# Last stage of a two-layer encoder: outputs in other PSUM banks, two scatters in one sum, both halves scaled together

## Chip, cores and metric

The kernel runs on one core of one Trainium2 chip. The metric is the device time of one execution in microseconds (us); lower is better. In one core five engines run side by side, each through its own list of instructions: TensorE (PE in the rows, its weight loads PEld), VectorE (DVE), ScalarE (ACT), GpSimd (POOL) and SyncE (SP), which issues the DMA transfers. They wait for each other through semaphores.

## The reference

The program is a trunk of two layers on 256 tokens of width 1024, in float32. The change concerns the very last part of the second layer, the mixture of experts: each token goes to 2 of 8 experts, and the weighted outputs are added to the residual `x`.

```python
def moe_swiglu(h, router, w1, w3, w2):
    logits = (t @ router)
    top_v, top_i = lax.top_k(logits, TOP_K)            # TOP_K = 2 of 8
    gates = jax.nn.softmax(top_v, axis=-1)
    combine = jnp.sum(jax.nn.one_hot(top_i, N_EXPERTS) * gates[..., None], axis=1)
    for e in range(N_EXPERTS):                         # w1, w3: 1024 x 3584, w2: 3584 x 1024
        out = out + combine[:, e:e + 1] * swiglu(t, w1[e], w3[e], w2[e])
...
x = x + moe_swiglu(h, router[f], moe_w1[f], moe_w3[f], moe_w2[f])
```

## The kernel before, in words

**Weights.** All weights are read from memory once, as a stream of units of 1 MB (`Stream`, L103): 128 partitions x 2048 numbers. SyncE issues the transfer into a `raw` buffer (7 of them). ScalarE rounds the unit into a high part `whi` (L135, 5 buffers), VectorE subtracts it from the unit and gets the low part `wlo` (L153, 4 buffers), and TensorE multiplies with both, so that the sum keeps float32 accuracy. `pieces` (L139) says whether the two do a unit in one instruction of 2048 numbers or in two of 1024; in the expert part (from unit `whole` on) it is one. The transfer of the stream's very last unit is already cut in two (L121). When TensorE has finished a unit, `release` (L162) asks for the subtraction 4 units ahead and the rounding 5 units ahead.

**Experts.** The tokens of an expert are gathered into up to 128 rows. A stage (L1076) computes the up projections (`h1`, `h3`) of one expert, chunk by chunk, and between them the down projection of the expert before (`down`, L1086), whose two output banks `y0` and `y1` hold 128 x 512 each. Two units are used for each of the 7 chunks of a down projection, so 14 units. For an expert with few tokens ("narrow", at most 64; the last one is) a unit takes 8 matmuls of 512 columns: 2 rows of blocks x (high, low) x (y0, y1). The last stage, `e == NE`, has no up projection: it is only the down projection of the last expert.

**Scatter.** `Back` (L1132) brings an expert's output back to its tokens. `scale` (L1140) multiplies a bank with the gate, on ScalarE into the high part `yh` (L1142) and on VectorE into the low part `yl` (L1143). `scatter` (L1146), for each half `i` of the 1024 columns and each block `b` of 128 tokens, makes two matmuls with the transposed one-hot matrix `pT` (yh at L1149, yl at L1150) and adds the bank to `x` on VectorE (L1151). In the last stage (L1197 to L1208) the scatters of the expert before are put behind the 4th and the 6th unit, and the last unit is done half by half: four matmuls into y0, then `final(0)`: scale, two scatters, two stores (L1153, 256 KB each) on SyncE; then the same for y1.

**PSUM.** The 8 banks are in three rings: four "mm" (`mm_bank`, for h1, h3), two "yd" (`yd_bank`, for y0, y1 and the scatters) and two "tp" (`tp_bank`, for transposes). A ring gives out its oldest bank, and who takes it waits until its last reader is done.

**Order.** In the expert part each engine works through its instructions in the order in which the code is written (`manual_schedule`, L1174); functions given to `in_units(n, fn)` run when n more units are done.

Of the kernel before, what the change touches and what calls it, by code (L numbers as in the profile page):

```python
# [11 lines left out]
F32 = mybir.dt.float32  # L12
F32R = mybir.dt.float32r
I32 = mybir.dt.int32
BF16 = mybir.dt.bfloat16
AF = mybir.ActivationFunctionType
OP = mybir.AluOpType
# [4 lines left out]
P = 128  # L22
D = 1024
KD = D // P
NT = 256
NB = NT // P
DFF = 2816
KF = DFF // P
NE = 8
# [13 lines left out]
GT = 15  # L43
# [26 lines left out]
def kernel(ctx: ExitStack, tc: tile.TileContext, x_in, positions, norm_mix, norm_ffn, conv_in,  # L70
                       conv_w, conv_out, attn_in, q_norm, k_norm, lam_q1, lam_k1, lam_q2, lam_k2, subln,
                       attn_out, ffn_w1, ffn_w3, ffn_w2, router, moe_w1, moe_w3, moe_w2, out):
    nc = tc.nc
    V, S, T = nc.vector, nc.scalar, nc.tensor
# [5 lines left out]
    work = ctx.enter_context(tc.tile_pool(name="work", bufs=2))  # L80
    psum = ctx.enter_context(tc.tile_pool(name="psum", bufs=4, space=PSUM))

    def mm_bank(name="mm"):
        return psum.tile([P, 512], F32, name=name, tag="mm", bufs=4)

    def yd_bank(name="yd"):
        return psum.tile([P, 512], F32, name=name, tag="yd", bufs=2)
# [4 lines left out]
    def tok(b):  # L92
        return slice(b * P, (b + 1) * P)
# [9 lines left out]
    class Stream:  # L103
        def __init__(self, units, whole=0):
            self.units = units
            self.whole = whole
            self.raw = {}
            self.high = {}
            self.spl = {}
            self.nd = 0  # L110
            self.nh = 0
            self.ns = 0
            self.done = 0
# [25 lines left out]
        def pieces(self, i):  # L139
            _, nk, nf = self.units[i]  # L140
            n = nk * nf
            step = n if i >= self.whole else n // 2
            return [slice(c, c + step) for c in range(0, n, step)]

        def split_to(self, j):
# [54 lines left out]
    ECH = DFE // 512  # L200
# [39 lines left out]
    x = const.tile([P, NB, D], F32)  # L240
    xf = x_in.rearrange("o (b p) d -> (o b) p d", p=P)
    outf = out.rearrange("o (b p) d -> (o b) p d", p=P)
# [124 lines left out]
    def proj(outs, xt, w, tsl, first, last, c0=0, cw=None):  # L367

        hi, lo = w
        cw = cw or hi.shape[2] // len(outs)  # L370
        nk = hi.shape[1]
        for kk in range(nk):
            *xs, c = xt(kk)
            a = xs[0][:, c, tsl]
            passes = [(a, hi), (a, lo)] + [(x[:, c, tsl], hi) for x in xs[1:]]
            for j, (l, m) in enumerate(passes):
                for i, o in enumerate(outs):
                    T.matmul(o, lhsT=l, rhs=m[:, kk, c0 + i * cw:c0 + (i + 1) * cw], start=first and kk + j == 0,  # L378
                             stop=last and kk == nk - 1 and j == len(passes) - 1)
# [4 lines left out]
    def chunked(tiles, k0):  # L384
        return lambda k: (*tiles[(k0 + k) // 4], (k0 + k) % 4)
# [59 lines left out]
    with ph1:  # L445
        hh, hl = hpair()
# [31 lines left out]
        for j in range(4):  # L478
# [5 lines left out]
            u = work.tile([P, 2, NT], F32, name="u", tag="w1")  # L484
# [13 lines left out]
            c = slice(2 * (j % 2), 2 * (j % 2) + 2)  # L498
            split(zt[j // 2][0][:, c, :], zt[j // 2][1][:, c, :], z)
            spare(2)  # L500
        u0 = 12
# [16 lines left out]
        hh, hl = hpair()  # L518
# [4 lines left out]
        for part, (n0, n1) in enumerate(FPARTS):  # L523
# [4 lines left out]
            hb, s1b, gt = {}, {}, {}  # L528
# [319 lines left out]
    def in_units(n, fn):  # L848

        pending.append([n, fn])  # L850
# [222 lines left out]
        in_units(2, turn)  # L1073
        return (gp,)

    def stage(s, u0, xs, gt, hooks=(), then=None):  # L1076


        narrow = xs is not None and len(xs) == 1
        hooks = dict(hooks)  # L1080
        full = slice(0, P)
        made = {}
        u = u0
        yb = []

        def down(n):  # L1086
            nonlocal u
            if gt is None:
                return
            if n == 0:  # L1090
                yb.extend([yd_bank("y0"), yd_bank("y1")])
            for i in range(2):
                end = (n, i) == (ECH - 1, 1)
                if end and then:
                    for half in range(2):
                        proj([yb[half]], chunked(gt, 4 * n + 2 * i), s.get(u), full, False, True, half * 512, 512)
                        then(half, yb[half])
                else:
                    proj(yb, chunked(gt, 4 * n + 2 * i), s.get(u), full, n + i == 0, end)
                u += 1  # L1100
                s.release()
                unit_done()

        for n in range(ECH):
            if xs is not None:
                h1, h3 = mm_bank("h1"), mm_bank("h3")
                for which, bank in ((1, h1), (3, h3)):
                    for half in range(2):
                        proj([bank], whole(xs, 4 * half), s.get(u), full, half == 0, half == 1)
                        u += 1  # L1110
                        if which == 1 and half == 1:
                            s1 = work.tile([P, 512], F32, name="s1", tag="w0")
                            S.activation(s1, h1, AF.Copy if narrow else AF.Silu)  # L1113
                        if which == 3 and half == 1:
                            if narrow:
                                s3 = work.tile([P, 512], F32, name="s3", tag="w0")
                                S.activation(s3, h3, AF.Copy)
                                made[n] = activate_narrow(s1, s3)
                            else:
                                made[n] = activate(s1, h3)  # L1120
                        s.release()
                        unit_done()
                        at = (n, 2 * (which // 3) + half)
                        if at in hooks:
                            hooks[at]()
            if n >= LAG:
                down(n - LAG)
        for n in range(ECH - LAG, ECH):
            down(n)
        return u, made, yb  # L1130

    class Back:  # L1132


        def __init__(self, pT, gate):
            self.pT, self.gate = pT, gate
            self.yh = work.tile([P, D], F32R, name="yh", tag="gain", bufs=1)
            self.yl = p3.tile([P, D], F32R, name="yl", tag="yl")

        def scale(self, i, bank):  # L1140
            c = slice(i * 512, (i + 1) * 512)
            S.activation(self.yh[:, c], bank, AF.Copy, scale=self.gate)  # L1142
            V.scalar_tensor_tensor(self.yl[:, c], bank, self.gate, self.yh[:, c].bitcast(F32), op0=OP.mult,  # L1143
                                   op1=OP.subtract)

        def scatter(self, b, i, bank_of=yd_bank, store=False):  # L1146
            c = slice(i * 512, (i + 1) * 512)
            bank = bank_of("sct")
            T.matmul(bank, lhsT=self.pT[:, tok(b)], rhs=self.yh[:, c], start=True, stop=False)  # L1149
            T.matmul(bank, lhsT=self.pT[:, tok(b)], rhs=self.yl[:, c], start=False, stop=True)  # L1150
            V.tensor_tensor(x[:, b, c], bank, x[:, b, c], op=OP.add)  # L1151
            if store:
                nc.sync.dma_start(outf[b][:, c], x[:, b, c])  # L1153

    pe = one_hot(0, slot1, rstds)
    with tc.issue_after(late["S"].ins), tc.issue_after(late["V"].ins):
# [1 line left out]
    xs = gather(pe)  # L1158
# [15 lines left out]
    with tc.manual_schedule(engines={ET.PE, ET.Activation, ET.DVE}):  # L1174
        for e in range(NE + 1):
            box = {}

            def back(b, last=last, bank_of=yd_bank):
                if last is not None:
                    for i in range(2):  # L1180
                        last.scatter(b, i, bank_of)

            def early(e=e):
                if e == 0:
                    some(gates())
                    some(rank_experts())

            def hot(e=e, pe=pe):
                backs[e] = route_back(pe, e, combr, in_units)
                if e + 1 < NE:  # L1190
                    box["pe"] = one_hot(e + 1, slot1 if is_wide(e + 1) else slotn, table=posr)

            def ahead(e=e):
                if e + 1 < NE:
                    box["x"] = gather(box["pe"], in_units) if is_wide(e + 1) else gather_narrow(box["pe"])

            def final(half, bank, box=box):  # L1197
                if half == 0:
                    box["y"] = Back(*backs.pop(NE - 1))
                box["y"].scale(half, bank)  # L1200
                for b in range(NB):
                    box["y"].scatter(b, half, mm_bank, store=True)

            if e == NE:
                in_units(4, lambda: back(0, bank_of=mm_bank))
                in_units(6, lambda: back(1, bank_of=mm_bank))
            u0, gt, yb = stage(st, u0, xs, gt, {(0, 0): early, (0, 3): lambda: back(0), (1, 3): lambda: back(1),
                                                (4, 0): hot, (5, 1): ahead}, final if e == NE else None)  # L1208
            if 0 < e < NE:
                last = Back(*backs.pop(e - 1))  # L1210
                for i in range(2):
                    last.scale(i, yb[i])
            pe, xs = box.get("pe"), box.get("x")
# [182 lines left out]
```

## Time and profile before

| | us |
|---|---|
| median of 3 runs (all: 1341.34, 1343.12, 1349.6) | 1343.12 |
| the profiled execution | 1343.34 |
| its span, first to last instruction | 1341.6 |
| mean granted TensorE clock, share of full speed | 0.993 |

The profile is of one execution. Rows give the start from the beginning of the span and the duration, both in us; x4 at the end of a row means four instructions in a row merged into one. An instruction's row tells the engine, the line of the kernel, the operation, and what is written from what is read, by the names in the program. In brackets stands the idle time of the engine just before, and whose result ended it. Matmul durations run from the start to the result; matmuls overlap, so the spacing of their starts tells the pace. A granted clock of 1.00 is 2.4 GHz, 0.50 is 1.2 GHz. The last stage takes the last 48 us of the span.

### The profile page before, as it was taken

What the parts mean: (1) busy time and instruction counts of PE and PEld (TensorE: products, weight loads), DVE (VectorE), ACT (ScalarE), POOL (GpSimd) and SP (SyncE); (2) the same over time, 40 slices, a digit from 0 to 9 for tenths busy, and PEclk for the clock granted to TensorE, in tenths of its full rate; (3) what the DMA queues carried; (4) which work ended last, traced back from release to release, by engine and by line L of the source; (5) the groups of instructions that cost most, each with busy time, mean ns of one, the idle gap of its engine ahead of it and who ended that gap; (6) DMA issues with size and microseconds to landing.
All of it is one profiled execution on the core that took longest, in us unless ns stands there. A gap on an engine that the chain in (4) does not pass through costs nothing. (4 is left out here: it accounts for less than half of the span.)

```text
span 1341.6 us, 17944 instructions
## 1 busy us (share of the span) xinstructions
PE 1303.6 (97%) x6539; PEld 1087.8 (81%) x6539; DVE 1138.6 (85%) x1216; ACT 944.5 (70%) x926; POOL 2.9 (0%) x12
## 2 busy tenths in 40 slices
PE   6999999999989999999999999999999999999987
PEld 6997888888767888888888888888888888888875
DVE  7967555557785898999998999998999999899986
ACT  5535444445774777987787988777988777798873
POOL 0000000000000000000000000000000000000000
PEclk9999999999999999999999999999999999999998
DMA  7954555546420899999999999999999999999992
GB/s 248 385 189 162 209 189 196 171 160 232 129 91 32 296 337 366 402 413 411 381 393 373 410 411 415 410 363 411 370 412 411 413 404 374 372 410 411 414 419 110
DMA packets 189150, 426.12 MB, mean 318 GB/s; under 512 B 8797, under 2 KB 23166, under 8 KB 189054
## 3 DMA queue, kind: packets, MB, share of 16 engines
q1 hardware_dynamic: 188622, 423.33, 83.8%
q0 software_dynamic: 432, 1.57, 0.3%
q8 instruction: 53, 0.87, 0.2%
q14 instruction: 43, 0.35, 0.1%
HBM read 423.82 MB, written 1.05 MB: 317 GB/s over the span
## 5 line engine op out<-in xcount | busy, mean ns | idle before, releaser
L153 DVE TENSOR_TENSOR wlo<-raw,whi 128x2048 fp32r<-128x2048 f32 (+1 forms) x466 | 908.0, 1990 | 80.6 <-issue 50.8
L135 ACT ACTIVATE whi<-raw 128x2048 fp32r<-128x2048 f32 (+1 forms) x466 | 768.7, 1675 | 235.8 <-PE h L378 91.0
L378 PE MATMUL h<-whi,xh 128*128 128x512 f32 x448 | 177.8, 397 | 0.0
L378 PE MATMUL h<-wlo,xp 128*128 128x512 f32 x448 | 175.4, 392 | 1.6 <-DVE wlo L153 1.5
L378 PE MATMUL h<-whi,xp 128*128 128x512 f32 x448 | 176.4, 394 | 0.0
L378 PE MATMUL h<-whi,xl 128*128 128x512 f32 x448 | 174.9, 390 | 0.0
L378 PE MATMUL h<-wlo,xh 128*128 128x512 f32 x448 | 174.7, 390 | 0.0
L378 PEld LDWEIGHTS h<-wlo,xp 128*128 128x128 f32 x448 | 84.2, 188 | 21.3 <-DVE wlo L153 4.1
L378 PEld LDWEIGHTS h<-whi,xl 128*128 128x128 f32 x448 | 84.2, 188 | 18.2
L378 PEld LDWEIGHTS h<-whi,xp 128*128 128x128 f32 x448 | 84.2, 188 | 16.7
L378 PEld LDWEIGHTS h<-wlo,xh 128*128 128x128 f32 x448 | 84.3, 188 | 16.6
L378 PEld LDWEIGHTS h<-whi,xh 128*128 128x128 f32 x448 | 84.2, 188 | 16.6
L378 PE MATMUL y<-whi,gp 128*128 128x512 f32 x224 | 71.4, 398 | 3.8 <-DVE yl L1143 3.8
L378 PE MATMUL y<-wlo,gh 128*128 128x512 f32 x224 | 70.3, 395 | 2.5 <-DVE wlo L153 2.2
L378 PE MATMUL h<-wlo,hh 128*128 128x512 f32 (+1 forms) x192 | 72.4, 377 | 0.0
L378 PE MATMUL h<-whi,hh 128*128 128x512 f32 (+1 forms) x192 | 71.6, 373 | 0.2 <-ACT hh L99 0.2
L378 PE MATMUL y<-wlo,gp 128*128 128x512 f32 x224 | 71.0, 397 | 0.4 <-DVE wlo L153 0.3
L378 PE MATMUL h<-whi,hl 128*128 128x512 f32 (+1 forms) x192 | 71.3, 372 | 0.0
L378 PE MATMUL y<-whi,gh 128*128 128x512 f32 x224 | 71.0, 398 | 0.0
L378 PE MATMUL y<-whi,gl 128*128 128x512 f32 x224 | 69.1, 390 | 0.0
L1113 ACT ACTIVATE s<-h 128x512 f32<-128x512 f32 x56 | 33.3, 595 | 33.7 <-PE h L378 33.7
L1060 PEld LDWEIGHTS tp<-fold,s 128*128 128x128 f32 x448 | 54.3, 192 | 2.2
(268 smaller groups left out, 1775.4 us busy)
## 6 DMA issues: line engine op xcount, KB each, us to landing
raw<-in_moe_w_dram SPq DMA_DIRECT2D x335, 1024.0 KB, 8.2
raw<-in_ffn_w_dram SPq DMA_DIRECT2D x33, 1024.0 KB, 4.9
raw<-in_conv_in_dram SPq DMA_DIRECT2D x12, 1024.0 KB, 10.2
raw<-in_attn_in_dram SPq DMA_DIRECT2D x12, 1024.0 KB, 5.1
raw<-in_conv_out_dram SPq DMA_DIRECT2D x4, 1024.0 KB, 12.1
raw<-in_attn_out_dram SPq DMA_DIRECT2D x4, 1024.0 KB, 7.0
x<-in_x_dram SPq DMA_DIRECT2D x2, 512.0 KB, 4.4
gain<-in_norm_ffn_dram POOLq DMA_DIRECT2D x2, 512.0 KB, 5.0
```

Source lines behind the costliest of these rows:

```text
L135: S.activation(hi[:, c], self.raw[i][:, c], AF.Copy)
L153: V.tensor_tensor(lo[:, c], r[:, c], hi[:, c].bitcast(F32), op=OP.subtract)
L378: T.matmul(o, lhsT=l, rhs=m[:, kk, c0 + i * cw:c0 + (i + 1) * cw], start=first and kk + j == 0, stop=last and kk == nk - 1 and j == len(pa ...
L1060: T.matmul(tp[:, o:o + NARROW], lhsT=h[:, c * P:(c + 1) * P], rhs=fold, start=True, stop=True)
L1113: S.activation(s1, h1, AF.Copy if narrow else AF.Silu)
```

## The change

It does six things, all in the last stage:

- `y0` and `y1` of the last stage are taken from the ring of the transposes (`tp_bank`) and no longer from the "yd" ring.
- The scatters of the expert before are written into four "mm" banks named `end`, one for each block and half, by a new `spread` that makes the two matmuls without an add; the sum is left open.
- The last unit is multiplied into y0 and y1 in turn, as all others are, and no longer half by half.
- Both halves are then scaled, one behind the other, into four separate tiles of 128 x 512 (`Back` with `final=True`, in the ring of the transposed activations).
- The last expert's spreads add onto the same four `end` banks; one add to `x` and one store follow for each bank.
- The last unit of a stream is rounded and subtracted in two pieces of 1024.

```diff
@@ Stream.pieces
-            step = n if i >= self.whole else n // 2
+            step = n if self.whole <= i < len(self.units) - 1 else n // 2
@@ stage
-    def stage(s, u0, xs, gt, hooks=(), then=None):
+    def stage(s, u0, xs, gt, hooks=(), bank_of=yd_bank):
...
-                yb.extend([yd_bank("y0"), yd_bank("y1")])
+                yb.extend([bank_of("y0"), bank_of("y1")])
             for i in range(2):
-                end = (n, i) == (ECH - 1, 1)
-                if end and then:
-                    for half in range(2):
-                        proj([yb[half]], chunked(gt, 4 * n + 2 * i), s.get(u), full, False, True, half * 512, 512)
-                        then(half, yb[half])
-                else:
-                    proj(yb, chunked(gt, 4 * n + 2 * i), s.get(u), full, n + i == 0, end)
+                proj(yb, chunked(gt, 4 * n + 2 * i), s.get(u), full, n + i == 0, (n, i) == (ECH - 1, 1))
@@ Back
+            if final:
+                self.y = [[p3.tile([P, 512], F32R, name=f"y{k}7", tag="g3", bufs=GT) for k in "hl"] for _ in range(2)]
+                return
...
+        def spread(self, b, i, bank, first=True, last=True):
+            yh, yl = self.y[i]
+            T.matmul(bank, lhsT=self.pT[:, tok(b)], rhs=yh, start=first, stop=False)
+            T.matmul(bank, lhsT=self.pT[:, tok(b)], rhs=yl, start=False, stop=last)
@@ the loop over experts
-            def final(half, bank, box=box):
-                if half == 0:
-                    box["y"] = Back(*backs.pop(NE - 1))
-                box["y"].scale(half, bank)
-                for b in range(NB):
-                    box["y"].scatter(b, half, mm_bank, store=True)
+            ends = {}
+
+            def spread_first(b, last=last, ends=ends):
+                for i in range(2):
+                    ends[b, i] = mm_bank("end")
+                    last.spread(b, i, ends[b, i], last=False)
 
             if e == NE:
-                in_units(4, lambda: back(0, bank_of=mm_bank))
-                in_units(6, lambda: back(1, bank_of=mm_bank))
+                in_units(4, lambda: spread_first(0))
+                in_units(6, lambda: spread_first(1))
             u0, gt, yb = stage(st, u0, xs, gt, {(0, 0): early, (0, 3): lambda: back(0), (1, 3): lambda: back(1),
-                                                (4, 0): hot, (5, 1): ahead}, final if e == NE else None)
+                                                (4, 0): hot, (5, 1): ahead}, tp_bank if e == NE else yd_bank)
+            if e == NE:
+                end = Back(*backs.pop(NE - 1), final=True)
+                for i in range(2):
+                    end.scale(i, yb[i])
+                for i in range(2):
+                    c = slice(i * 512, (i + 1) * 512)
+                    for b in range(NB):
+                        end.spread(b, i, ends[b, i], first=False)
+                        V.tensor_tensor(x[:, b, c], ends[b, i], x[:, b, c], op=OP.add)
+                        nc.sync.dma_start(outf[b][:, c], x[:, b, c])
```

VectorE in the last stage, before (y_10281 is the second half of the expert before, y_10878 and y_10879 are the two halves of the last expert):

```order
L1143 SCALAR_TENSOR_TENSOR yl<-y_10281,gate,yh 128x512
L153 TENSOR_TENSOR wlo<-raw,whi 128x2048 x4
L1151 TENSOR_TENSOR x<-sct,x 128x512 x2
L153 TENSOR_TENSOR wlo<-raw,whi 128x2048 x2
L1151 TENSOR_TENSOR x<-sct,x 128x512 x2
L153 TENSOR_TENSOR wlo<-raw,whi 128x2048 x4
L1143 SCALAR_TENSOR_TENSOR yl<-y_10878,gate,yh 128x512
L1151 TENSOR_TENSOR x<-sct,x 128x512 x2
L1143 SCALAR_TENSOR_TENSOR yl<-y_10879,gate,yh 128x512
L1151 TENSOR_TENSOR x<-sct,x 128x512 x2
```

And the same engine and place in the changed kernel, whose line numbers differ:

```order
L1141 SCALAR_TENSOR_TENSOR yl<-y_10281,gate,yh 128x512
L153 TENSOR_TENSOR wlo<-raw,whi 128x2048 x9
L153 TENSOR_TENSOR wlo<-raw,whi 128x1024 x2
L1141 SCALAR_TENSOR_TENSOR yl_11052<-y_10878,gate,yh_11051 128x512
L1141 SCALAR_TENSOR_TENSOR yl_11054<-y_10879,gate,yh_11053 128x512
L1216 TENSOR_TENSOR x<-end,x 128x512 x4
```

The four adds between the wlo are gone, the tenth wlo is two pieces, and the two yl of the last expert stand together ahead of all four adds.

TensorE from the last unit on, before (in brackets the engines whose semaphores an instruction waits for):

```order
L378 MATMUL y_10878<-whi,gp 128x512 [waits Activation_49]
L378 MATMUL y_10878<-wlo,gp 128x512 [waits DVE_49]
L378 MATMUL y_10878<-whi,gp 128x512
L378 MATMUL y_10878<-wlo,gp 128x512
L1149 MATMUL sct<-yh,pT 128x512 [waits Activation_49]
L1150 MATMUL sct<-yl,pT 128x512 [waits DVE_49]
L1149 MATMUL sct<-yh,pT 128x512
L1150 MATMUL sct<-yl,pT 128x512
L378 MATMUL y_10879<-whi,gp 128x512
L378 MATMUL y_10879<-wlo,gp 128x512
L378 MATMUL y_10879<-whi,gp 128x512
L378 MATMUL y_10879<-wlo,gp 128x512
```

And in the changed kernel, from the second half of the last unit on:

```order
L378 MATMUL y_10878<-whi,gp 128x512 [waits Activation_49]
L378 MATMUL y_10879<-whi,gp 128x512
L378 MATMUL y_10878<-wlo,gp 128x512 [waits DVE_49]
L378 MATMUL y_10879<-wlo,gp 128x512
L1145 MATMUL end<-yh_11051,pT 128x512 [waits Activation_49]
L1146 MATMUL end<-yl_11052,pT 128x512 [waits DVE_49]
L1145 MATMUL end<-yh_11051,pT 128x512
L1146 MATMUL end<-yl_11052,pT 128x512
L1145 MATMUL end<-yh_11053,pT 128x512 [waits Activation_49]
L1146 MATMUL end<-yl_11054,pT 128x512 [waits DVE_49]
L1145 MATMUL end<-yh_11053,pT 128x512
L1146 MATMUL end<-yl_11054,pT 128x512
```

The last four matmuls into y_10879 no longer stand behind the first half's scatters, and all eight scatter matmuls come at the end. The eight of the expert before stay where they were, behind the 4th and the 6th unit.

## Rows read from the trace of the kernel before

**Rows 1.** The page: busy time of each engine, share of the span, instructions.
```profile
PE 1303.6 (97%) x6539; PEld 1087.8 (81%) x6539; DVE 1138.6 (85%) x1216; ACT 944.5 (70%) x926; POOL 2.9 (0%) x12
```

**Rows 2.** The chain that ended last, in order of time: start, us, what.
```profile
1297.46 0.75 DVE yl L1143
...
1312.55 7.27 PE y L378 x32
...
1319.85 6.30 DVE wlo L153 x3
...
1327.20 0.69 ACT yh L1142
...
1330.32 1.72 PE y L378 x4
...
1333.59 0.51 PE sct L1150
```

**Rows 3.** Timeline around the start of the last stage, VectorE and TensorE.
```profile
1285.39 0.43 DVE L1067 TENSOR_TENSOR gn<-tp,s1n 128x256 f32<-128x256 f32 x1
...
1293.57 2.29 DVE L153 TENSOR_TENSOR wlo<-raw,whi 128x2048 fp32r<-128x2048 f32 x1 [0.43 <-PE y L378]
...
1296.79 1.41 DVE L1143 SCALAR_TENSOR_TENSOR yl<-y,gate,yh 128x512 fp32r<-128x512 f32 x2
...
1297.60 0.49 PE L378 MATMUL y<-whi,gp 128*128 128x512 f32 x1 [3.67 <-DVE yl L1143]
...
1301.64 8.90 DVE L153 TENSOR_TENSOR wlo<-raw,whi 128x2048 fp32r<-128x2048 f32 x4 [3.44 <-PE y L378]
```

**Rows 4.** Timeline of the middle of the last stage, ScalarE and VectorE.
```profile
1303.05 5.56 ACT L135 ACTIVATE whi<-raw 128x2048 fp32r<-128x2048 f32 x3 [0.30 <-PE y L378]
...
1310.46 1.28 DVE L1151 TENSOR_TENSOR x<-sct,x 128x512 f32<-128x512 f32 x2
...
1311.66 4.48 DVE L153 TENSOR_TENSOR wlo<-raw,whi 128x2048 fp32r<-128x2048 f32 x2
...
1316.06 1.28 DVE L1151 TENSOR_TENSOR x<-sct,x 128x512 f32<-128x512 f32 x2
...
1317.26 8.89 DVE L153 TENSOR_TENSOR wlo<-raw,whi 128x2048 fp32r<-128x2048 f32 x4
```

**Rows 5.** Timeline of VectorE near the kernel's start: two wlo of 1024.
```profile
26.70 2.35 DVE L153 TENSOR_TENSOR wlo<-raw,whi 128x1024 fp32r<-128x1024 f32 x2
```

**Rows 6.** Timeline of the end: first half's scatters, second half's adds.
```profile
1328.73 0.74 PE L1150 MATMUL sct<-yl,pT 128*128 128x512 f32 x1 [0.29 <-DVE yl L1143]
...
1329.26 0.63 PE L1149 MATMUL sct<-yh,pT 128*128 128x512 f32 x1
...
1329.69 0.63 PE L1150 MATMUL sct<-yl,pT 128*128 128x512 f32 x1
...
1334.13 1.29 DVE L1151 TENSOR_TENSOR x<-sct,x 128x512 f32<-128x512 f32 x2 [0.59 <-PE sct L1150]
```

**Rows 7.** Table by stretch; its first row here names the columns.
```profile
core 0: us, PE busy (x) PEld busy (x) DVE busy (x) ACT busy (x) POOL busy (x), PEclk, DMA share, GB/s
1297.50:1299.50 2.00, 1.74 (x4) 1.24 (x5) 0.70 (x2) 0.00 (x0) 0.00 (x0) 0.65 1.03 424
...
1301.50:1305.00 3.50, 3.50 (x17) 2.87 (x16) 3.36 (x2) 3.20 (x3) 0.00 (x0) 1.00 1.02 420
...
1315.00:1320.00 5.00, 5.00 (x24) 4.14 (x23) 5.00 (x5) 4.50 (x3) 0.00 (x0) 1.00 0.00 1
...
1326.00:1328.00 2.00, 1.02 (x4) 0.55 (x4) 0.22 (x2) 0.69 (x1) 0.00 (x0) 1.00 0.00 0
...
1329.00:1330.00 1.00, 1.00 (x3) 0.81 (x3) 0.50 (x1) 0.00 (x0) 0.00 (x0) 0.50 0.00 0
...
1331.00:1332.00 1.00, 1.00 (x3) 0.30 (x1) 0.05 (x1) 0.00 (x0) 0.00 (x0) 0.50 0.75 277
...
1336.00:1338.00 2.00, 0.00 (x0) 0.00 (x0) 0.00 (x0) 0.00 (x0) 0.00 (x0) 0.50 0.62 218
```

More of the change, by code (lines that the diff above doesn't have):

```diff
@@ L1132, with __init__, scatter @@
     class Back:
-        def __init__(self, pT, gate):
+        def __init__(self, pT, gate, final=False):
             self.pT, self.gate = pT, gate
-            self.yh = work.tile([P, D], F32R, name="yh", tag="gain", bufs=1)
-            self.yl = p3.tile([P, D], F32R, name="yl", tag="yl")
-        def scale(self, i, bank):
-            c = slice(i * 512, (i + 1) * 512)
[L1142 to L1150, printed above, removed]
+            if final:
+                self.y = [[p3.tile([P, 512], F32R, name=f"y{k}7", tag="g3", bufs=GT) for k in "hl"] for _ in range(2)]
+                return
+            yh = work.tile([P, D], F32R, name="yh", tag="gain", bufs=1)
+            yl = p3.tile([P, D], F32R, name="yl", tag="yl")
+            self.y = [[t[:, i * 512:(i + 1) * 512] for t in (yh, yl)] for i in range(2)]
+        def scale(self, i, bank):
+            yh, yl = self.y[i]
+            S.activation(yh, bank, AF.Copy, scale=self.gate)
+            V.scalar_tensor_tensor(yl, bank, self.gate, yh.bitcast(F32), op0=OP.mult, op1=OP.subtract)
+        def spread(self, b, i, bank, first=True, last=True):
+            yh, yl = self.y[i]
+            T.matmul(bank, lhsT=self.pT[:, tok(b)], rhs=yh, start=first, stop=False)
+            T.matmul(bank, lhsT=self.pT[:, tok(b)], rhs=yl, start=False, stop=last)
+        def scatter(self, b, i):
+            c = slice(i * 512, (i + 1) * 512)
+            bank = yd_bank("sct")
+            self.spread(b, i, bank)
             V.tensor_tensor(x[:, b, c], bank, x[:, b, c], op=OP.add)
-            if store:
-                nc.sync.dma_start(outf[b][:, c], x[:, b, c])
     pe = one_hot(0, slot1, rstds)
@@ L1176, with back @@
             box = {}
-            def back(b, last=last, bank_of=yd_bank):
+            def back(b, last=last):
                 if last is not None:
                     for i in range(2):
-                        last.scatter(b, i, bank_of)
+                        last.scatter(b, i)
             def early(e=e):
```

## The prediction

> **What bounds the kernel now.** I read the page first, then the chain of waits, then the timeline and the table by stretch of the last 50 us, because the diff touches only the last stage: the down projection of the last expert (14 weight units, called units 1 to 14 here), the scatters of the last two experts, and the stores. Over the whole span TensorE is busy 97% and VectorE 85% [rows 1], but such shares say nothing of one stage. The chain that ended last does [rows 2]. In the last stage it runs: VectorE's yl of the expert before, then TensorE's down projection, then from 1319.85 VectorE's wlo subtractions (three in 6.30 us, the last done at 1326.15), then a strict hand-over between ScalarE, VectorE and TensorE, once for each half of the output: yh at 1327.20, second half of y at 1330.32, and the last adds, 1334.13 + 1.29 = 1335.42 [rows 2, 6]. So there are three places. (a) The start: TensorE stands still for 3.67 us, from 1293.93 to 1297.60, waiting for yl, since y0 and y1 need the two banks that yh and yl are still read from; VectorE's next wlo, which needs a buffer of unit 1, stands still for 3.44 us and begins at 1301.64 [rows 3]. (b) The middle: VectorE is the pace, ten wlo and four adds without a gap, 1301.64 to 1326.15 [rows 2 to 4]. ScalarE needs 5.56 / 3 = 1.85 us a unit and is not the pace [rows 4]. (c) The end: 1326.15 to 1335.42, 9.27 us in which two halves go through the same hand-over one behind the other.
>
> **(a) y0 and y1 in the transposes' banks.** Nothing is computed more or less. The last reader of a transpose bank is the gn at 1285.39 (0.43 us) [rows 3], 8 us before TensorE is ready; the last expert's remaining transposes are done by then, since no up projection follows. So TensorE goes on at about 1293.8. Units 1 to 4 have their wlo by 1293.57 + 2.29 = 1295.86 [rows 3], the last of them for a unit that begins three units later. VectorE then splits gp and does the two yl, as before, until 1296.79 + 1.41 = 1298.20, and finds unit 1's buffer free: eight matmuls at 7.27 / 32 = 0.227 us [rows 2] end at 1295.6. Its fifth wlo thus starts at 1298.20 in place of 1301.64: 3.44 us. TensorE's stretch at the lower clock after the pause (granted 0.65 on average in 1297.5 to 1299.5, against 1.00 in 1301.5 to 1305) [rows 7] should go as well. A new wait: the first spread, behind unit 4, needs yh and yl of the expert before. TensorE is there at 1293.8 + 32 x 0.227 = 1301.1, yl is done at 1298.20, so 2.9 us of other units cover it; behind it stands only unit 5.
>
> **(b) One sum in one bank.** The eight scatter matmuls of the expert before stay, into four "mm" banks that nothing else asks for in this stage. The four adds between the wlo go: 1311.66 - 1310.46 = 1.20 us twice [rows 4] = 2.40 us of VectorE's chain. The ten wlo took 24.51 - 2.40 = 22.11, 2.21 each. Cutting the last in two costs little: two pieces of 1024 took 2.35 us [rows 5], one whole 2.29 [rows 3], so 0.06. On ScalarE the extra instruction hides, as it has 0.36 us a unit to spare. The new end of wlo: 1298.20 + 9 x 2.21 = 1318.1 for unit 13, 1319.3 and 1320.45 for the halves of unit 14. Now TensorE has to be asked: 14 x 8 + 8 = 120 matmuls at 0.227 are 27.2 us, from 1293.8 to 1321.0. It waits only at unit 13 (its first wlo matmul could start at 1317.85, wlo comes at 1318.1: 0.25). So the last of them ends at about 1321.3: VectorE's saving (1326.15 to 1320.45, 5.7 us) is nearly all real, but TensorE takes over as the bound by some 0.5 us, and the cut in two hardly counts. The weights don't: in 1315 to 1320 the DMA moved 1 GB/s, so all had landed by 1315 [rows 7], and unit 14's whi is wanted at about 1317.2. Were that cover gone, each us of lateness would cost one.
>
> **(c) Both halves together.** Unit 14 begins on TensorE at 1319.5, the last matmul into y0 is its seventh, 6 x 0.227 = 1.36 later, and its result comes between 0.23 (the spacing) and 0.51 us (a scatter behind a wait [rows 2]) later: y0 is complete at about 1321.25. Then yh0 (0.69 [rows 2]) to 1322.0, both yl (1.41 [rows 3]) to 1322.75 and 1323.4, with yh1 beside them. The first yl matmul starts at 1322.8; seven spreads remain. At the full clock (1.00, 2.4 GHz) the last ends at 1322.8 + 0.51 + 6 x 0.227 = 1324.7 and VectorE's adds are the bound: four from 1323.4, 0.60 each behind one another (1.29 for two [rows 6]), 1325.9. At the half clock (0.50, 1.2 GHz), as the same matmuls ran before, the first three take from 1328.73 to 1329.69 + 0.63, 1.59 us, and the others 0.43 each [rows 6]: 1326.1, and the last add ends at 1326.8. Before, the clock was still 1.00 in 1326 to 1328 and 0.50 in 1329 to 1330 [rows 7], some us behind the first gaps, so either can come; I take the middle, 1326.3. The last add is then 1335.42 - 1326.3 = 9.1 us earlier: 3.4 from (a), 2.3 from (b), 3.4 from (c).
>
> **The stores** come in one row of four, not two and two. Behind the last add lay 1341.6 - 1335.42 = 6.2 us before. The trace has no four in a row. The bounds: 262 KB at 218 GB/s (1336 to 1338) or 277 (1331 to 1332) [rows 7] are 1.2 or 0.95 us, against 0.6 to 0.7 between the issues; three queue up 0.9 to 1.5 us, where the second of a pair queued 0.3 to 0.5: 0.6 to 1.0 more. From the other side 0, if four move faster than two did. The rows are nearest to the upper bound for the queue and to neither for the rate; I take 0.5.
>
> **Sum.** 9.1 - 0.5 = 8.6 us. The profiled execution took 1343.34 (span 1341.6 and 1.7 around it); 1343.34 - 8.6 = 1334.7. Its time lies 0.2 above the median of 1343.12, which changes nothing. That is 0.6%, less than the 1% that a measurement of this kernel can about tell from no change.
>
> **Rivals.**
> 1. The change does not do what it says at (a): some wait keeps TensorE off the transposes' banks, and the pause stays. For it: the new first matmuls still carry waits on ScalarE and VectorE. Against: the last reader is 8 us earlier [rows 3]. Then 3.44 come back: 1338.2.
> 2. The end crowds: half clock for the spreads (1326.8) and the upper bound of the store queue (1.0): 1335.7.
> 3. The other side: the clock. TensorE loses its long pause, but is held up in short ones by wlo, and if these make its clock fall within the stage, TensorE becomes the bound: 8 x 0.43 = 3.44 us a unit. If it falls from unit 9 on (at 1310.1, six units, 20.6 us) the last matmul comes at 1330.7 in place of 1321.3, and the time is 1344.1: that is the point from which it decides. From unit 5 on it is 1351.5; over all 120 matmuls (51.6 us) 1358.8, 1.2% slower. For it: this very stage shows 0.65 [rows 7]. Against: that came behind 3.67 us of standing still; between 1326 and 1328, with TensorE busy 1.02 of 2.00 us, the clock was 1.00, and in 1315 to 1320, busy throughout, too [rows 7].
> The Trainium skill has a rule for this rival (TensorE: Matmul & The Clock Gate, section "A second HAM failure mode: psum-queue depth-cycling"): a TensorE that goes round PSUM banks and idles briefly but often between groups of matmuls can swing between its two rates, and throughput suffers. By that rule the time would lie between 1344.1 and 1358.8, without it at 1334.7; the trace so far bears it out only at the end (0.50 in 1329 to 1330), not within the stage, so it stays the small chance it has.
> 4. More than I see: full clock to the end and no store queue, 1343.34 - 9.5 = 1333.8; beyond that VectorE's ten wlo and TensorE's 120 matmuls both bar the way, and a gain over 13.4 us (1%) would need something outside this stage.
>
> **How the numbers follow.** Forecast with its near variants (1333.8 to 1335.5) 0.72; rival 2 0.12; rival 1 0.06; rival 3 0.05, most of it within 1%; rival 4's unknown part 0.05. The three runs of before spread over 8 us, and a median can move 2 or 3 us by itself, so the range goes from 1330.5 (forecast less such a shift) to 1340.0 (rival 1 and the same). Faster by over 1% (under 1329.7) takes rival 4's part, 0.05; slower by over 1% (over 1356.6) the far end of rival 3, 0.03; within 1% the rest, 0.92.
>
> **What would show it.** In the new profile: TensorE's y matmuls without a pause behind the expert before and at a granted clock of 1.00; the fifth wlo at about 1298.2, eleven wlo in one row, ending near 1320.5; the last y matmul near 1321.3; four adds in a row ending near 1326.3; some 6.7 us from there to the span's end, at 1333.0. I am wrong on (a) if a wait of some us on yl or gn stands before y0, on (b) if gaps open between the wlo (late weights or buffers), on (c) if more than 5.5 us lie between the last y matmul and the last add, on the clock if 0.50 shows before 1321, and in the tail if it exceeds 7.5 us.

## The result and the profile after

The changed kernel took 1335.11 us (median of 10 runs, 1333.67 to 1343.13), the kernel before 1343.42 (10 runs, 1341.34 to 1351.35, the three shown above among them). The ratio is 0.994, with a 95% interval of 0.9922 to 0.9958: 8.1 us less, between 5.6 and 10.5. Forecast were 1334.7 and 8.6 less. A second measurement (e10_changed_again below) gave 1337.75 (12 runs) against 1343.16 (21 runs), a ratio of 0.9952 (0.9934 to 0.9971): 6.4 us less, between 3.9 and 8.9.

The profiled execution of the changed kernel took 1339.28 (span 1337.5), 4 us above its median. It came late to the last stage: TensorE's last result for the expert before is there at 1298.82 (in the row below, 1298.20 + 0.62), in the kernel before at 1293.92. The length of the stage does not hang on that: the same kernel profiled again (e10) began it at 1294.19 and was through with the last add 31.97 us later, here 32.05. So from here on times are counted from this point, the start of the stage. It took 1341.6 - 1293.92 = 47.7 us before and 1337.5 - 1298.82 = 38.7 after: 9.0 us less.

TensorE in the last stage, from the timeline of the changed kernel:

```profile
1298.20 0.62 PE L378 MATMUL y<-whi,gl 128*128 128x512 f32 x2
1298.65 0.61 PE L378 MATMUL y<-whi,gp 128*128 128x512 f32 x2
...
1323.05 0.73 PE L378 MATMUL y<-wlo,gp 128*128 128x512 f32 x2 [0.20 <-DVE wlo L153]
...
1325.90 0.61 PE L378 MATMUL y<-wlo,gp 128*128 128x512 f32 x2
1327.07 0.49 PE L1145 MATMUL end<-yh,pT 128*128 128x512 f32 x1 [0.55 <-ACT yh L1140]
1327.85 0.50 PE L1146 MATMUL end<-yl,pT 128*128 128x512 f32 x1 [0.29 <-DVE yl L1141]
...
1329.36 0.40 PE L1146 MATMUL end<-yl,pT 128*128 128x512 f32 x1
```

The pause of 3.67 us [rows 3] is gone: the last expert's first matmul follows 0.45 us behind the start of the pair before it. Up to the end of the down projection there is one wait on the engine, at unit 13: 0.20 us of idle time, by which that matmul starts 0.37 late (0.25 was forecast). The last eight spreads, apart from the first two, which wait for yh and yl, run at a spacing of 0.23, not 0.43 as in [rows 6].

VectorE in the same stretch:

```profile
1301.68 1.41 DVE L1141 SCALAR_TENSOR_TENSOR yl<-y,gate,yh 128x512 fp32r<-128x512 f32 x2 [0.15 <-ACT yh L1140]
1303.01 22.25 DVE L153 TENSOR_TENSOR wlo<-raw,whi 128x2048 fp32r<-128x2048 f32 x11
1327.05 1.41 DVE L1141 SCALAR_TENSOR_TENSOR yl<-y,gate,yh 128x512 fp32r<-128x512 f32 x2 [1.79 <-ACT yh L1140]
1328.39 2.48 DVE L1216 TENSOR_TENSOR x<-end,x 128x512 f32<-128x512 f32 x4
```

Eleven wlo stand in one row where before there were three rows with adds between them [rows 4], and the row begins right behind yl, not 3.44 us later [rows 3]. It ends at 1325.26, 26.4 us after the start of the stage; before it was 32.2. The four adds take 2.48 and end at 1330.87, 32.05 us after the start; before it was 41.5 [rows 6].

The table by stretch, with the columns of [rows 7]:

```profile
1297.50:1299.50 2.00, 2.00 (x10) 1.66 (x9) 1.66 (x2) 1.41 (x2) 0.00 (x0) 1.00 1.04 426
...
1301.50:1305.00 3.50, 3.50 (x17) 2.88 (x16) 3.35 (x4) 3.50 (x4) 0.00 (x0) 1.00 1.02 419
...
1315.00:1320.00 5.00, 5.00 (x24) 4.14 (x23) 5.00 (x3) 3.82 (x3) 0.00 (x0) 1.00 0.82 337
...
1326.00:1328.00 2.00, 1.16 (x5) 0.43 (x4) 0.95 (x2) 1.27 (x2) 0.00 (x0) 1.00 0.00 0
1328.00:1329.00 1.00, 1.00 (x5) 0.81 (x6) 1.00 (x2) 0.00 (x0) 0.00 (x0) 1.00 0.02 8
...
1330.00:1331.00 1.00, 0.00 (x0) 0.00 (x0) 0.88 (x2) 0.00 (x0) 0.00 (x0) 1.00 0.95 350
```

The granted clock is 1.00 (2.4 GHz) in the first 6 us of the stage, where it had fallen to 0.65, and also during the last spreads, where it had been 0.50. The four stores begin to move in 1330 to 1331 at 350 GB/s. That is not a higher rate than before: the windows with 277 and 218 hold time in which little moved, and in 1332.0 to 1332.5 the first pair of before moved at 389. From the last add to the end of the span it is 6.6 us, against 6.2. SyncE's rows of issues, first before, then changed:

```profile
1330.22 6.36 SPq L1153 DMA_DIRECT2D out_dram<-x  x4
```

```profile
1329.11 3.37 SPq L1217 DMA_DIRECT2D out_dram<-x  x4
```

The last issue ends at 1336.58 before, 1.16 us behind the last add, and at 1332.48 in the changed kernel, 1.61 behind it; from there to the end of the span it is 5.0 us in both.

The chain of waits of the changed kernel, cut to this stage, shows who is now last:

```profile
1307.52 11.12 DMA raw<-in_moe_w_dram
...
1318.75 1.93 ACT whi L135
...
1320.70 2.30 DVE wlo L153
...
1323.05 3.26 PE y L378 x13
...
1326.33 0.70 ACT yh L1140
...
1327.05 1.41 DVE yl L1141 x2
...
1328.46 1.83 DVE x L1216 x3
```

It now goes back through unit 13's wlo and whi to the arrival of its weights. VectorE's row has no gap there, so this cost next to nothing (22.25 us for eleven wlo, 22.17 in e3_half_by_half below); but weights, VectorE and TensorE now come within half a us of each other, which no term of the forecast had said of the weights of unit 13. ScalarE shows why, as it waits for the transfers:

```profile
1316.27 1.92 ACT L135 ACTIVATE whi<-raw 128x2048 fp32r<-128x2048 f32 x1 [0.62 <-DMA raw<-in_moe_w_dram]
1318.75 3.81 ACT L135 ACTIVATE whi<-raw 128x2048 fp32r<-128x2048 f32 x3 [0.56 <-DMA raw<-in_moe_w_dram]
```

A unit of weights comes every 2.5 us, VectorE needs 2.2 for one. The weights land some 21 us after the start of the stage in both kernels (by 1315 before, by about 1320 here), but the changed kernel wants them earlier. By these numbers a still shorter row on VectorE would wait for them; no run tried one.

### The profile page after: what moved, and what is told of

Read it like the earlier page. It is cut to its first block, busy times and chain, and to the rows that moved or that the text cites. A ratio compares the mean times of both kernels' runs of the same rounds, so it can differ in the third digit from the quotient of the medians.

```text
span 1337.5 us, 17941 instructions
## 1 busy us (share of the span) xinstructions
PE 1305.2 (98%) x6539; PEld 1089.9 (81%) x6539; DVE 1136.0 (85%) x1213; ACT 947.9 (71%) x927; POOL 2.9 (0%) x12
## 4 chain that ended last, share of the span: by engine, by line
PE 93%; DVE 4%; ACT 1%; DMA 1%; issue 0%; DVEq 0%; ACTq 0%
PE h L378 46%; PE y L378 18%; PE yd L378 8%; PE qkv L378 5%; PE tp L1060 4%; DVE wlo L153 2%; PE tp L358 2%; PE mm L471 2%; PE mm L472 2%; PE mm L470 2%; PE tp L889 1%; PE tp L904 1%; DMA raw<-in_moe_w_dram 1%; PE sc L647 1%; PE tp L677 1%; PE tp L550 0%
## 5 line engine op out<-in xcount | busy, mean ns | idle before, releaser
L1107 ACT ACTIVATE s<-h 128x512 f32<-128x512 f32 x56 | 33.3, 594 | 31.6 <-PE h L378 31.4
```

## The experiments

All compute the whole reference. What is compared is the last stage, from TensorE's last result for the expert before; the yh column gives the start of the first yh of the last expert, which stands 0.03 us behind y0's last result (for e8 and e9 that of the second half). The tail is the end of the span less the end of the last add. Each row is one profile. Up to the last add the changed kernel was profiled three times (changed, e10, and e7, which differs only in the stores): 32.05, 31.97, 31.97. Its tail differs more, 6.6 and 7.0.

| kernel | stage begins at | to yh | to the last add's end | to the end of the span | tail | us, whole run |
|---|---|---|---|---|---|---|
| before | 1293.92 | 33.3 | 41.50 | 47.7 | 6.2 | 1343.34 |
| changed | 1298.82 | 27.5 | 32.05 | 38.7 | 6.6 | 1339.28 |
| e1_old_banks | 1293.25 | 33.0 | 37.50 | 44.7 | 7.2 | 1339.71 |
| e2_adds_back | 1299.07 | 29.8 | 34.38 | 41.3 | 7.0 | 1342.19 |
| e3_half_by_half | 1293.40 | 27.0 | 33.75 | 39.8 | 6.1 | 1334.98 |
| e4_last_unit_whole | 1292.77 | 28.3 | 32.85 | 40.0 | 7.2 | 1334.57 |
| e5_banks_alone | 1294.00 | 29.7 | 37.70 | 44.0 | 6.3 | 1339.81 |
| e6_one_sum_alone | 1302.07 | 32.1 | 38.87 | 44.9 | 6.1 | 1348.86 |
| e7_two_queues | 1293.81 | 27.4 | 31.97 | 38.4 | 6.4 | 1334.06 |
| e8_by_columns | 1299.35 | 32.3 | 35.68 | 41.9 | 6.2 | 1342.95 |
| e9_by_columns_late | 1293.26 | 29.3 | 32.62 | 38.7 | 6.1 | 1333.81 |
| e10_changed_again | 1294.19 | 27.4 | 31.97 | 39.0 | 7.0 | 1335.0 |

The last column shows why single whole times would have misled here: e6 is 5.5 us slower than the kernel before as a whole and 2.8 faster in the stage, because its stage began 8 us late.

**Undoing one edit at a time.** First the banks:

```diff
-                                                (4, 0): hot, (5, 1): ahead}, tp_bank if e == NE else yd_bank)
+                                                (4, 0): hot, (5, 1): ahead}, yd_bank)
```

> The changed kernel with one edit undone: y0 and y1 of the last stage again from the ring of the scatters. Measured is the last stage: from the result of TensorE's last matmul for the expert before to the end of the span, 47.7 us in the kernel before and 38.7 in the changed one. Theory (each part of the change took away a wait of its own, so parts add up): TensorE's pause of 3.7 us behind yl and the stretch at the lower clock come back, VectorE's fifth wlo starts 3.4 us later, and the stage takes 42.1. Rival (TensorE and VectorE are level in this stage, so a wait taken from one is mostly given back by the other): under 40.2.

It took 44.7: neither. The pause is back, and VectorE's row starts behind 3.45 us of idle time, as the theory has it. But TensorE loses more than that, as its timeline and the clock show:

```profile
1292.64 0.61 PE L378 MATMUL y<-whi,gl 128*128 128x512 f32 x2
1296.93 0.49 PE L378 MATMUL y<-whi,gp 128*128 128x512 f32 x1 [3.67 <-DVE yl L1141]
1297.59 0.79 PE L378 MATMUL y<-whi,gp 128*128 128x512 f32 x1 [0.17 <-DVE yl L1141]
1298.18 1.05 PE L378 MATMUL y<-wlo,gp 128*128 128x512 f32 x2
...
1300.74 0.72 PE L378 MATMUL y<-whi,gp 128*128 128x512 f32 x2
```

```profile
1296.50:1300.00 3.50, 2.91 (x7) 2.12 (x8) 1.03 (x2) 0.16 (x1) 0.00 (x0) 0.64 1.03 422
```

Eight matmuls stand between 1296.93 and 1300.74, 3.81 us in place of 8 x 0.227 = 1.82. With the pause of 3.67 that is 5.7 us, and since TensorE then waits for no other engine up to the end of the down projection, 5.45 of it reaches the last add (37.50 against 32.05). So the banks are worth the pause and the slow stretch behind it, where TensorE sets the pace.

Then the adds between the wlo:

```diff
-                    last.spread(b, i, ends[b, i], last=False)
+                    last.spread(b, i, ends[b, i])
+                    V.tensor_tensor(x[:, b, c], ends[b, i], x[:, b, c], op=OP.add)
...
-                        end.spread(b, i, ends[b, i], first=False)
+                        ends[b, i] = mm_bank("end2")
+                        end.spread(b, i, ends[b, i])
```

> The changed kernel with the four adds of the expert before put back between the wlo (its scatters close their sums, the last expert's go to fresh sums in the same ring). Theory: VectorE's row of wlo ends 2.4 us later; TensorE uses the last piece 0.6 us after it is there, so 1.8 us reach the end: 40.5. Rival (the adds lay beside TensorE's work, the gain there is nil): 38.7 to 39.2.

The last add came 2.33 us later (34.38): the theory, but with nearly all of the adds' 2.4 rather than 1.8. With a tail 0.3 longer the stage took 41.3, 0.8 more than expected. VectorE and TensorE:

```profile
1312.07 1.28 DVE L1203 TENSOR_TENSOR x<-end,x 128x512 f32<-128x512 f32 x2
...
1317.67 1.28 DVE L1203 TENSOR_TENSOR x<-end,x 128x512 f32<-128x512 f32 x2
```

```profile
1321.20 0.73 PE L378 MATMUL y<-wlo,gp 128*128 128x512 f32 x2 [1.29 <-DVE wlo L153]
```

Behind the second pair of adds TensorE stands 1.29 us for a wlo, which it did not in the changed kernel: with the adds VectorE is the pace, without them TensorE.

Then the halves, the last unit and its hand-over as in the kernel before, but with the sums and banks of the changed one:

```diff
-                proj(yb, chunked(gt, 4 * n + 2 * i), s.get(u), full, n + i == 0, (n, i) == (ECH - 1, 1))
+                if then and (n, i) == (ECH - 1, 1):
+                    for half in range(2):
+                        proj([yb[half]], chunked(gt, 4 * n + 2 * i), s.get(u), full, False, True, half * 512, 512)
+                        then(half, yb[half])
+                else:
+                    proj(yb, chunked(gt, 4 * n + 2 * i), s.get(u), full, n + i == 0, (n, i) == (ECH - 1, 1))
```

> The changed kernel with the last unit again half by half, each half scaled, spread, added and stored before the next. Theory (two hand-overs one behind the other): 3.4 us more at the end, 0.4 less behind the last add as only two stores stand there: 41.7. Rival (the second half's matmuls ran beside the first half's hand-over, and what it cost before was only the lower clock, four matmuls at 0.43 in place of 0.23): 39.5 to 40.

39.8: the rival's number. The last add came only 1.70 us later, and 0.6 of that is given back in the tail, where two stores stand and not four. But the rival's reason is not the whole of it. ScalarE's two yh, and the clock:

```profile
1320.35 0.69 ACT L1145 ACTIVATE yh<-y,gate 128x512 fp32r<-128x512 f32 x1 [4.20 <-PE y L378]
1323.80 0.69 ACT L1145 ACTIVATE yh<-y,gate 128x512 fp32r<-128x512 f32 x1 [2.77 <-PE y L378]
```

```profile
1322.00:1324.00 2.00, 1.76 (x7) 1.11 (x7) 1.29 (x2) 0.20 (x1) 0.00 (x0) 1.00 0.01 5
```

Half by half, yh starts 0.56 us earlier (26.95 against 27.51), as y0 need not wait for y1's matmuls; from there to the last add it takes 6.80 in place of 4.54, at a clock of 1.00 throughout. In the kernel before, the same stretch took 1335.42 - 1327.20 = 8.22, with the clock at 0.50 in its first part [rows 7]: 1.4 us of its end were the clock. All of them lie between the two yh (4.86 us before, 3.45 in e3), where the matmuls ran at a spacing of 0.43 and here at 0.23; behind the second yh both take the same time.

Last the cut of the last unit, undone:

```diff
-            step = n if self.whole <= i < len(self.units) - 1 else n // 2
+            step = n if i >= self.whole else n // 2
```

> The changed kernel with the last unit rounded and subtracted in one piece again. Theory (TensorE, not VectorE, is the bound there by about half a us): 0.2 us more, 38.9. Rival (the end hangs on wlo): half a wlo, 1.1 us more, 39.8.

The last add came 0.80 us later, the stage took 40.0 with a tail that was longer, too. That is nearer to the rival. TensorE stood 0.35 us for the whole wlo of unit 14: its first matmul with it starts 26.84 us after the start of the stage, in the changed kernel 26.17. Only 0.20 of this difference is VectorE's wait for a late whi:

```profile
1317.26 2.29 DVE L153 TENSOR_TENSOR wlo<-raw,whi 128x2048 fp32r<-128x2048 f32 x1 [0.20 <-ACT whi L135]
```

```profile
1319.61 0.73 PE L378 MATMUL y<-wlo,gp 128*128 128x512 f32 x2 [0.35 <-DVE wlo L153]
```

**One edit alone, on the kernel before.** The banks:

```diff
-                yb.extend([yd_bank("y0"), yd_bank("y1")])
+                yb.extend([bank_of("y0"), bank_of("y1")])
```

> The kernel before with one edit alone: y0 and y1 of the last stage from the ring of the transposes; adds, halves and the whole last unit as before. Read off are two times from the result of TensorE's last matmul for the expert before: to y0 complete (33.25 us in the kernel before) and to the end of the span (47.7). Theory (with the adds in its row VectorE is the pace, so only its 3.4 us count): y0 after 29.8, the end after 44.3. Rival (TensorE is the pace, as in the changed kernel, where undoing the banks cost 5.5): y0 after 27.8 to 28.3. If the clock at the end stays at 1.00, as it did in e3_half_by_half, another 1.5 to 2 us go from the end.

y0 after 29.7, the end after 44.0: the theory. The same edit that costs 5.45 to undo in the changed kernel gives 3.8 here (41.50 to 37.70), because with the adds in its row VectorE is the pace and TensorE's slow stretch is hidden behind it. TensorE waits for unit 11's wlo, the first behind the adds, and the clock falls again in the hand-overs:

```profile
1316.12 0.74 PE L378 MATMUL y<-wlo,gp 128*128 128x512 f32 x2 [1.29 <-DVE wlo L153]
```

```profile
1324.00:1326.00 2.00, 1.25 (x4) 0.79 (x5) 0.95 (x2) 0.41 (x1) 0.00 (x0) 0.91 0.00 0
1326.00:1328.00 2.00, 2.00 (x6) 1.31 (x4) 1.18 (x2) 0.00 (x0) 0.00 (x0) 0.50 0.32 121
```

The sums; beside e3, the banks and the whole last unit are the old ones:

```diff
-            step = n if self.whole <= i < len(self.units) - 1 else n // 2
+            step = n if i >= self.whole else n // 2
...
-                                                (4, 0): hot, (5, 1): ahead}, tp_bank if e == NE else yd_bank,
+                                                (4, 0): hot, (5, 1): ahead}, yd_bank,
```

> The kernel before with one edit alone: the scatters of the last two experts in one sum, four adds fewer in VectorE's row; banks of y0 and y1, halves and the whole last unit as before. First theory (the parts add up): y0 is complete 2.4 us earlier, 30.9 us after the start of the stage. Rival (without the adds TensorE is the pace, held up by its pause and the clock behind it; e1_old_banks had y0 after 32.9): y0 after 32.7 to 33.0, nearly nothing gained by this edit alone.

y0 came after 32.0, 1.2 us earlier than before: between the two, and the reason is the rival's. Behind its pause TensorE waits for nobody up to y0, so it is the pace and takes part of VectorE's saving. The rival's figure was too high because it came from e1, where the last matmul into y0 is the seventh of the last unit and not the fourth, 0.7 us later. The last add came 2.6 earlier, as the clock did not fall in the hand-over this time:

```profile
1305.74 1.45 PE L378 MATMUL y<-whi,gp 128*128 128x512 f32 x2 [3.67 <-DVE yl L1146]
```

```profile
1336.00:1338.00 2.00, 1.55 (x7) 0.94 (x5) 1.29 (x2) 0.41 (x1) 0.00 (x0) 1.00 0.11 41
```

**The tail, and a version meant to beat both.** Stores in turn from two queues:

```diff
-                        nc.sync.dma_start(outf[b][:, c], x[:, b, c])
+                        (nc.sync if b else nc.scalar).dma_start(outf[b][:, c], x[:, b, c])
```

> The changed kernel with its four stores issued in turn by ScalarE and SyncE in place of SyncE alone. The tail from the end of the last add to the end of the span was 6.2 us before, 6.6 to 7.2 with four stores in a row. Theory (the stores queue behind each other at the issue): 6.2. Rival (they queue in the transfer, or the tail is spent behind them): 6.6 to 7.2 as before.

6.4: between the two, 0.2 below the shortest tail of four stores from one queue (6.6, the others 7.0 to 7.2). One profile can't tell that from chance.

The last expert's weights by columns, so that the first half's work lies beside the second half's matmuls:

```diff
-    units += stage_units((), w2)
+    units += [cols(w2, half * 512, 512, 4 * n, 4) for half in range(2) for n in range(ECH)]
...
+            for half in range(2):
+                yb.append(bank_of(f"y{half}"))
+                for n in range(ECH):
+                    proj([yb[half]], chunked(gt, 4 * n), s.get(u), full, n == 0, n == ECH - 1)
...
+                then(half, yb[half])
```

> A version meant to beat both: the last expert's down weights are cut by columns (7 units for y0, then 7 for y1), so that the first half is scaled and spread beside the second half's matmuls; its two adds and stores come in the gap before the second half's yl, and only the second half's hand-over, two adds and two stores stand at the end. Theory: one yl more in VectorE's row (0.66) costs 0.5 at the last matmul, two adds and one yl fewer behind it gain 1.1, two stores fewer gain 0.4 to 1.0: the stage takes 37.4 in place of 38.7. Rival (VectorE's row was the bound after all): 38.4 or more.

41.9: the rival's number, but not its reason, as the fault is where the first half's scatters stand. TensorE stood for yh and yl, which come late, as yl stands behind seven wlo in VectorE's row, and behind that wait the clock fell:

```profile
1319.19 0.50 PE L1155 MATMUL end<-yh,pT 128*128 128x512 f32 x1 [1.70 <-ACT yh L1150]
```

```profile
1319.17 0.75 DVE L1151 SCALAR_TENSOR_TENSOR yl<-y,gate,yh 128x512 fp32r<-128x512 f32 x1
```

```profile
1320.00:1322.00 2.00, 2.00 (x5) 1.61 (x6) 2.00 (x1) 2.00 (x3) 0.00 (x0) 0.50 0.30 117
```

So they were moved three units back, and the changed kernel itself was run beside it, unedited:

```diff
-                    in_units(2, lambda: [ended[0].spread(b, 0, ends[b, 0], first=False) for b in range(NB)])
+                    in_units(5, lambda: [ended[0].spread(b, 0, ends[b, 0], first=False) for b in range(NB)])
```

> e8_by_columns with the first half's scatters moved on TensorE from behind unit 9 to behind unit 12, since in e8 TensorE stood there for yh and yl, which VectorE and ScalarE reach only behind the wlo of unit 11 and the whi of unit 12. Theory (that wait was all that e8 lost): the last add ends 31.4 us after the start of the stage (32.05 in the changed kernel), two stores leave a tail of 6.1 in place of 6.6 to 7.2, and the stage takes 37.5 in place of 38.7; the time, 1 us of 1335, can't be told from the changed kernel's. Rival (VectorE's longer row is the bound): 38.7 or more.

> The changed kernel itself, beside e9 on the same chip: 38.7 us for the stage and a ratio to the kernel before of 0.994; its place within the spread of runs follows whether the clock falls between 380 and 420 us (0.83 or 0.74 in the profiles that came late to the last stage, 1.00 in the others).

That wait went, but another came: the one yl more in VectorE's row delays the next wlo, and TensorE stands for that.

```profile
1313.07 0.75 DVE L1151 SCALAR_TENSOR_TENSOR yl<-y,gate,yh 128x512 fp32r<-128x512 f32 x1
1313.74 6.75 DVE L153 TENSOR_TENSOR wlo<-raw,whi 128x2048 fp32r<-128x2048 f32 x4
```

```profile
1316.08 0.50 PE L378 MATMUL y<-wlo,gp 128*128 128x512 f32 x1 [0.84 <-DVE wlo L153]
```

The second half's yh starts 29.3 us after the start of the stage (27.4 in the changed kernel), the last add ends at 32.62; the shorter tail makes up for it, and the stage takes 38.7, as in the changed kernel (38.7 and 39.0). Of the 1.8 us by which yh is later, this wait is 0.84; another 0.9 are the four spreads (4 x 0.227) that TensorE now does ahead of it. So the rival's number came, and its reason holds for about half: VectorE's row has no room for a yl, although it was no longer the bound, and TensorE's has none for four matmuls. The times agree: 0.9951 of the kernel before (0.9928 to 0.9974), and 0.9952 (0.9934 to 0.9971) for the changed kernel on the same chip. No version found beats it.

## Why the prediction was right

- **The sum.** Forecast 8.6 us; measured 8.1 (5.6 to 10.5) and, the second time, 6.4 (3.9 to 8.9); 9.0 in the stage of the profile (8.7 in e10). That the first median came within half a us of the forecast is in part luck, as two medians of one kernel lie 2.6 us apart. The last add was forecast 9.1 earlier and came 9.4 earlier. The forecast took its terms from three stretches of VectorE's row, and these came out as worked out: the start of the row 3.5 us earlier (3.4 forecast), the row 2.3 shorter (2.3), from its end to the last add 5.6 in place of 9.3, 3.7 less (3.4). What was wrong is which edit gives how much. A path of kernels that differ by one step shows that: before 41.50, banks (e5) 37.70, then sums and the cut (e3) 33.75, then both halves together (changed) 32.05. As prices of the edits, two of the three terms were mis-sized, in opposite directions.
- **(a), the banks: 3.4 forecast, 3.8 measured** as the first step. TensorE goes on at once, and VectorE's fifth wlo starts 4.2 us after the start of the stage, as worked out (1298.20 less 1293.93). Only the slow stretch that "should go as well" had no number in it: where TensorE is the pace, the step is worth 5.45 (e1), 2 us more than forecast.
- **(b), one sum: 2.3 forecast, 3.95 measured** with the cut. The adds' 2.4 reach the end (e2: 2.33). The term was too small because it did not have the clock: e5 still ran part of its two hand-overs at 0.50, e3 ran the same two at 1.00, 7.97 us from the first yh to the last add in the one and 6.80 in the other. Each is one profile; the kernel before (0.50) and e6 (1.00) agree with them. "The cut in two hardly counts" was wrong: 0.80 in e4. By the forecast's own times a whole wlo of unit 14 would be there at 1318.1 + 2.21 = 1320.3, and TensorE wants it two matmuls into the unit, at 1319.5 + 0.45 = 1319.95; the forecast compared VectorE's end with TensorE's last matmul and not with the first that needs this wlo. The statement that the weights don't bind failed, too, but cost less: 0.20 in e4.
- **(c), both halves together: 3.4 forecast, 1.7 measured.** The term took the whole of 9.27 us as the price of two hand-overs. Some 1.4 of it was the clock, which the earlier steps had by then given back, and half by half lets y0's yh start 0.56 earlier.
- **The clock at the end:** the middle between 1325.9 and 1326.8 was taken; it stayed at 1.00 and the last add came at 32.05 after the start, which is 1326.0 on the scale of the forecast.
- **The stores:** 0.5 more was taken; 0.4 in the profile of the result, 0.8 to 1.0 in e1, e2, e4 and e10, against tails of 6.1 to 6.3 us for all kernels with two stores at the end. The bounds held; the rate that carried the upper one did not, as the 218 and 277 GB/s held time in which little moved. Of the longer tail 0.45 to 0.7 us lie in the issues: the last one ends 1.6 to 1.8 us behind the last add with four stores from one queue, 1.1 to 1.35 with two. From there it is 4.9 to 5.4 us to the end in all. Why the issues take longer was not tried.
- **The rivals.** The pause did not stay. Rival 3's clock did not fall in the changed kernel, and in e2, with a wait of 1.29 us for one wlo and 0.10 in each of the next two units, it stayed at 1.00, too. It fell behind the pause of 3.67 us (the kernel before, e1, e6), in e8 behind waits of 1.70 and 0.28 us, and at the end of the kernel before and of e5, where waits for wlo are followed by two hand-overs. The rule of the Trainium skill that was weighed there (TensorE: Matmul & The Clock Gate, "A second HAM failure mode: psum-queue depth-cycling": short idle times between groups of matmuls can make the rate swing) is borne out by these two ends only in part: the same two hand-overs ran at 1.00 in e3 and e6, and short waits for wlo alone did not bring it about in any run here.

## What to carry to other kernels

Before pricing a change by the wait that it removes, ask which engine sets the pace after it: the same move to other banks was worth 3.8 us while VectorE was the pace and 5.45 once TensorE was, and the same hand-over by halves 1.7 rather than 3.4. Here a pause of the matmul engine cost the pause (3.67) and 2.0 us of slow matmuls behind it, and an engine that had ceased to be the bound by half a us had no room for one more instruction of 0.75 (e9). Where runs of one kernel spread by more than the change is worth, compare the stage from its own start, not the whole.

## What the runs showed of the chip

Whether TensorE's clock falls in the attention, between 380 and 420 us, decides the place of a run within the spread, in the twelve executions that were profiled. None of the kernels here differs in that stretch. The last stage began at 1292.8 to 1294.2 in all eight profiles with 1.00 there, at 1298.8 to 1299.4 in the three with 0.83, and at 1302.1 in the one with 0.74. The first row is of the changed kernel, the second of the same kernel run again (e10), the third of e6:

```profile
380.00:420.00 40.00, 36.23 (x171) 25.69 (x170) 22.91 (x85) 25.11 (x84) 0.00 (x0) 0.83 0.16 53
```

```profile
380.00:420.00 40.00, 35.70 (x197) 25.77 (x195) 27.36 (x91) 27.97 (x89) 0.00 (x0) 1.00 0.19 61
```

```profile
380.00:420.00 40.00, 36.26 (x160) 24.92 (x159) 21.09 (x74) 25.08 (x82) 0.00 (x0) 0.74 0.16 53
```

TensorE is idle for about a tenth of that stretch in all three, and in 380 to 385, at the end of which the clock falls in two of them, it is busy for 2.50 of the 5 us in each. The same instructions are granted the full clock in one run and 1.2 GHz for a part of the time in another, and lose 5 or 8 us by it: at 353 us (the first matmuls of L677) the three are within 0.3 us of each other, at the last of L677 they are at 411.2 (e10), 416.2 (changed) and 419.4 (e6). That is as much as the whole change brought. What makes it fall in one run and not in another stays open.
